# A decoder layer on one core: another form of its first two products, of its norms' sums and of its last norm's order

## The chip, the cores and the metric

The kernel runs on one core of a Trainium2 chip. The metric is the device time of one execution in microseconds (us). The engines are PE (TensorE: PE are its matmuls, PEld its weight loads), DVE (VectorE), ACT (ScalarE), POOL (GpSimd) and SP (SyncE, which here only issues DMAs). An engine takes its instructions in order and waits on semaphores for the others.

## What is computed

One layer of a decoder, for 256 prompt tokens and 8 x 4 sample tokens that share the weights (288 tokens in all, D = 2048):

```python
z = x @ w_in                       # h, gate_b, gate_c, q, k, v, g_a, g_b in one product
ya = gate_b * conv3(gate_c * h)
yb = dilated sliding-window attention(q, k, v), 3 groups of 4 heads
mixed = sigmoid(g_a) * (ya @ w_branch_a) + sigmoid(g_b) * (yb @ w_branch_b)
x1 = layernorm(ALPHA * x + mixed @ w_out, ln1_g, ln1_b)
a, b = split(x1 @ w_up)            # D_FF = 5632
y = layernorm(ALPHA * x1 + (silu(conv3(a)) * b) @ w_down, ln2_g, ln2_b)
```

`layernorm` takes mean and variance over the 2048 features of a token. Besides y the kernel returns the new caches and convolution states. All is f32.

## The kernel before, in words

Features lie on the 128 partitions, tokens in the columns: a [2048, 288] array is 16 tiles ("k") of [128, 288]. A weight block is a [2048, 128] piece of a weight matrix (1 MB), in SBUF [128, 16, 128]. A product of a block with the activations is 48 matmuls of 288 columns: both operands are split into a high part (rounded to the type F32R) and the rest, and for each k the three matmuls high x high, high x low and low x high are summed in PSUM (`mms`, L188 to L197). So a block has to be split before it is used: ACT copies it to `whi` (L137), DVE subtracts (`wlo`, L138), each in two halves of 8 tiles (`half_block`). `whi` and `wlo` have 4 half buffers each, the raw block `wst` 3 buffers.

`product` (L174) takes the split block at the head of a list, loads and splits the next one (`prepare`, L161), and returns the PSUM tile ("acc", 5 buffers). The layer is a long row of such products: 12 for q, 24 for k and v, 48 for the convolution branch, then gates, branches, w_out (16), and the FFN in three parts of 16, 16 and 12 tiles (up: two products a tile; down: 16 products a part). Attention and the work on the sample caches are put between them. The code is written in program order; a tile framework works out the semaphores, and a scheduler that simulates the times decides the order of each engine's instructions.

The start (L209 to L239): 20 matmuls of a zero tile (`N_WARM`, L212). x is loaded by ACT's queue in four pieces (`FIRST` = tiles 0-1, 2-7, 8-11, 12-15), the first two weight blocks of w_in by SP's queue, per piece first block 0, then block 1. Each piece is split as it comes (L234, L235 for weights, L200, L201 for x: `split`). The two products on them are ordinary calls of `product`. There are 8 semaphores for DMAs from these queues in turn, so the ninth DMA is issued when the first has landed. The constants `cst`, `m_dist` and the parameters `prm` are loaded in the loop over q at j == 0 (L436 to L438), that is behind the second and third block. `m_dist` lies in the array "yal".

The norms (class `Norm`, L542 to L631). dd holds the 16 tiles that are to be normalised. For tile 0, `first` gets c, the mean of tile 0's features per token, from a matmul with the constant `ones_p` (1/128; L552, an f32 matmul) and subtracts it; c is taken off all other tiles too, which keeps the sums small. `add(i)` squares a tile on ACT (L560) and adds it and its square into s1 and s2 on POOL (L564, L565). For the last tile, four f32 matmuls with `ones_d` (1/2048) sum s1, s2 and the last tile and its square over the partitions (L572, L573). At tile 14 a dummy Ln loads ACT's table ahead (L568).

`finish` (first norm, L578) computes mean, v = variance + EPS and r = exp(-0.5 ln v), with one Newton step, in SBUF tiles `lw`; the normalisation is folded into the FFN's first part (`normed`, L654), whose products read the activations unnormalised and run on while the statistics are made. `finish_out` (last norm, L593) ends the kernel: DVE and POOL share the 16 tiles, subtract the mean (`MEAN_DVE`, `MEAN_POOL`), multiply by r (`OUT_DVE`, `OUT_POOL`, L604), then ACT (L630), or DVE for the tiles in `OUT_LAST` (L628), applies g and b, and SP stores the tiles in six DMAs (`OUT_ORDER`, L631).

Of the kernel before, what the change touches and what calls it, by code (L numbers as in the profile page):

```python
# [11 lines left out]
F32R = mybir.dt.float32r  # L12
AF = mybir.ActivationFunctionType
ALU = mybir.AluOpType
# [3 lines left out]
P = 128  # L18
D = 2048
KD = D // P  # L20
# [3 lines left out]
T = SEQ + NS  # L24


H = T // 2
# [4 lines left out]
HK = KD // 2  # L32
# [18 lines left out]
C_M0 = C_TM + NT  # L51
# [11 lines left out]
N_CT = 18  # L63
N_REST = 48

FIRST = ((0, 2), (2, 6), (8, 4), (12, 4))

N_WARM = 20


N_STEP = N_CT + 2
N_STEP_BLOCKS = 2 * NG * NH + 5 * KD - 3

MEAN_DVE = ((0, 3), (3, 3), (6, 3))
MEAN_POOL = ((9, 1), (10, 2), (12, 2), (14, 2))
OUT_DVE = ((0, 1), (1, 3), (4, 3), (7, 4))
OUT_POOL = ((11, 1), (12, 2), (14, 2))
OUT_ORDER = ((0, 1), (1, 3), (4, 3), (7, 4), (11, 3), (14, 2))
OUT_LAST = (9, 10, 11, 12, 13)


@with_exitstack
def layer_kernel(ctx: ExitStack, tc: tile.TileContext, ins, outs):
# [14 lines left out]
    def sb(pl, shape, tag, dt=F32, bufs=None):  # L98
        return pl.tile(shape, dt, tag=tag, name=nm(tag), bufs=bufs)

    def acc(half=H):
        return sb(ps, [P, half, 2], "acc")

    def h2(ap):
        return ap.rearrange("p (h a) -> p h a", h=2)

    def h3(ap):
        return ap.rearrange("p k (h a) -> p k h a", h=2)

    def att(cols=512):  # L110
        return sb(ps, [P, cols], "att", bufs=2)

    def f32(ap):
        return ap.bitcast(F32)
# [9 lines left out]
    def behind(i, after):  # L124

        tc.add_manual_dep(i.ins, after.ins.name, no_sync, reason="pace")
# [47 lines left out]
    def product(x):  # L174

        w = w_ready.pop(0)
        if not w_ready:
            prepare()
        if steps_on[0]:
            spent[0] += N_STEP  # L180
            while spent[0] >= N_STEP_BLOCKS:
                spent[0] -= N_STEP_BLOCKS
                next(steps, None)
        o = acc(x[0].shape[-1])
        mms(o, w, x)
        return o.rearrange("p a h -> p h a")
# [12 lines left out]
    def split(hi, lo, src):  # L199
        act.copy(hi, src)  # L200
        dve.tensor_tensor(lo, src, f32(hi), ALU.subtract)  # L201

    ones_d = sb(big, [P, P], "ones_d")
    ones_p = sb(big, [P, P], "ones_p")
    pool.memset(ones_d, 1.0 / D)
    pool.memset(ones_p, 1.0 / P)


    zero = sb(wk, [P, T], "cy", F32R, bufs=2)  # L209
# [7 lines left out]
    xl = sb(big, [P, KD, 2, HX], "xl", F32R)  # L217
    x_in = ins["x"].rearrange("p (k t) -> p k t", t=T)
    xs = sb(big, [P, KD, T], "yah")
    for k0, n in FIRST:  # L220
        act.dma_start(xs[:, k0 : k0 + n, :], x_in[:, k0 : k0 + n, :])
    w_ready = []
    stage = []
    for b in range(2):
        stage.append((sb(wp, [P, KD, P], "wst"), ins["w_in"][b].rearrange("p (k c) -> p k c", c=P)))
        halves = [[sb(wp, [P, HK, P], n, F32R, bufs=4) for n in ("whi", "wlo")] + [HK] for _ in range(2)]
        w_ready.append(halves)
    for k0, n in FIRST:
        k = slice(k0, k0 + n)
        h = slice(k0 % HK, k0 % HK + n)  # L230
        for b, (st, src) in enumerate(stage):
            sp.dma_start(st[:, k, :], src[:, k, :])
            hi, lo, _ = w_ready[b][k0 // HK]
            act.copy(hi[:, h, :], st[:, k, :])  # L234
            dve.tensor_tensor(lo[:, h, :], st[:, k, :], f32(hi[:, h, :]), ALU.subtract)  # L235
            if b == 0:
                split(xh[:, k, :, :H], xl[:, k, :, :H], h3(xs[:, k]))
    x = (xh[:, :, :, :H], xl[:, :, :, :H])
    x_gb = (xh[:, :, :, :HG], xl[:, :, :, :HG])  # L239

    cst = sb(big, [P, C_M0], "cst")

# [187 lines left out]


    kv = sb(big, [P, 2, 2, NG, T], "dd")
    for j in range(NH):
        for g in range(NG):
            act.copy(h2(q_all[:, j, g]), product(x))
            if j == 0 and g > 0:  # L436
                for dst, src in ((cst, ins["cst"][:, :C_M0]), (m_dist, ins["cst"][:, C_M0:])) if g == 1 else ((prm, ins["prm"]),):
                    behind(sp.dma_start(dst, src), w_load[0])  # L438
        pool.tensor_copy(q_s[:, :, j, :], q_all[:, j, :, SEQ:])
    steps_on[0] = True  # L440
    for j in range(NH):
# [100 lines left out]
    class Norm:  # L542


        def __init__(self, g, b):
            self.g, self.b = g, b
            self.s1, self.s2, self.c = (lw[:, k] for k in range(3))

        def first(self):

            p = att(T)
            pe.matmul(p, ones_p, dd[:, 0], start=True, stop=True)  # L552
            act.copy(self.c, p)
            dve.tensor_tensor(dd[:, 0], dd[:, 0], self.c, ALU.subtract)

        def add(self, i):
            d = dd[:, i]
            last = i == KD - 1
            q = self.s2 if i == 0 else sb(wk, [P, T], "cy", bufs=2)
            act.activation(q, d, AF.Square)  # L560
            if i == 0:
                pool.tensor_copy(self.s1, d)
            elif not last:
                pool.tensor_tensor(self.s1, self.s1, d, ALU.add)  # L564
                pool.tensor_tensor(self.s2, self.s2, q, ALU.add)  # L565
            if i == KD - 2:

                act.activation(lw[:, 3, 0:1], q[:, 0:1], AF.Ln)  # L568
            if last:
                self.p1, self.p2 = att(T), att(T)  # L570
                for p, s, e in ((self.p1, self.s1, d), (self.p2, self.s2, q)):
                    pe.matmul(p, ones_d, s, start=True, stop=False)  # L572
                    pe.matmul(p, ones_d, e, start=False, stop=True)  # L573

        def at(self, c, i):
            return prm[:, c + i : c + i + 1]
# [1 line left out]
        def finish(self):  # L578

            mu, v, r, t = (lw[:, k] for k in range(3, 7))  # L580
            act.copy(mu, self.p1)
            act.activation(t, self.p1, AF.Square)
            dve.scalar_tensor_tensor(v, self.p2, EPS, t, ALU.add, ALU.subtract)
            act.activation(t, v, AF.Ln)
            act.activation(r, t, AF.Exp, scale=-0.5)

            dve.tensor_tensor(t, r, r, ALU.mult)
            dve.scalar_tensor_tensor(t, t, -0.5, v, ALU.mult, ALU.mult)
            dve.scalar_tensor_tensor(r, t, 1.5, r, ALU.add, ALU.mult)
            dve.scalar_tensor_tensor(mu, mu, -1.0, r, ALU.mult, ALU.mult)  # L590
            self.r, self.nmr = r, mu

        def finish_out(self, y, out):  # L593

            mu, r_pool, t = (lw[:, k] for k in range(3, 6))
            mean, v = self.p1, self.p2
            r, dev = (sb(ps, [P, T], tag, bufs=n) for tag, n in (("acc", None), ("long", 1)))
            act.activation(t, mean, AF.Square)
            act.copy(mu, mean)
            i_v = dve.scalar_tensor_tensor(v, v, EPS, t, ALU.add, ALU.subtract)  # L600

            def by_token(eng, k0, n, w, op):
                k = slice(k0, k0 + n)
                return eng.tensor_tensor(dd[:, k], dd[:, k], w.unsqueeze(1).broadcast_to([P, n, T]), op)  # L604

            for k0, n in MEAN_POOL:
                by_token(pool, k0, n, mu, ALU.subtract)
            act.activation(t, v, AF.Ln)
            act.activation(r, t, AF.Exp, scale=-0.5)
            with tc.issue_after(i_v.ins):  # L610
                for k0, n in MEAN_DVE:
                    i_m = by_token(dve, k0, n, mean, ALU.subtract)

            act.activation(t, r, AF.Square)
            with tc.issue_after(i_m.ins):
                dve.scalar_tensor_tensor(t, t, -0.5, v, ALU.mult, ALU.mult)
                i_r = dve.scalar_tensor_tensor(dev, t, 1.5, r, ALU.add, ALU.mult)
            act.copy(r_pool, dev)
            for k0, n in OUT_POOL:
                by_token(pool, k0, n, r_pool, ALU.mult)  # L620
            with tc.issue_after(i_r.ins):
                for k0, n in OUT_DVE:
                    i_m = by_token(dve, k0, n, dev, ALU.mult)
            for k0, n in OUT_ORDER:
                for i in range(k0, k0 + n):
                    if i in OUT_LAST:
                        with tc.issue_after(i_m.ins):
                            dve.tensor_scalar(y[:, i], dd[:, i], self.at(self.g, i), self.at(self.b, i), ALU.mult, ALU.add)  # L628
                    else:
                        act.activation(y[:, i], dd[:, i], AF.Identity, bias=self.at(self.b, i), scale=self.at(self.g, i))  # L630
                sp.dma_start(out[:, k0 : k0 + n, :], y[:, k0 : k0 + n, :])  # L631


    n1 = Norm(R_LN, R_LN + KD)
    for i in range(KD):
        o = product((h3(mxh), h3(mxl)))
        xf = sb(wk, [P, T], "h", bufs=2)
# [25 lines left out]

    cf = sb(big, [P, KF, 2 + 2 * NB], "qk_s")
    f = 0
    n2 = Norm(R_LN + 2 * KD, R_LN + 3 * KD)
    for part, nf in enumerate(THIRDS):
        gh = sb(big, [P, KD, T], "yah", F32R)
        gl = sb(big, [P, KD, T], "yal", F32R)
# [229 lines left out]
```

## Time and profile before

| | |
|---|---|
| runs, us | 1770.14, 1771.77, 1772.48; median 1771.77 |
| the profiled execution, us | 1772.71 |
| its span (first to last instruction), us | 1770.9 |
| mean granted TensorE clock | 0.995 |
| moved by DMA | 436.25 MB, mean 246 GB/s |
| PE matmuls L194, L195, L196 on x, busy us | 940.1, 936.3, 937.3 (3264 each) |
| DVE L138 (low parts of blocks) | 710.5 us, 580 x 1225 ns |
| ACT L137 (high parts of blocks) | 592.3 us, 580 x 1022 ns |

The times of the views are counted from the span's start; the execution's own time is 1.8 us more than the span. A group's row gives line, engine, operation, out<-in tiles, and in brackets the idle time of the engine ahead of it with what ended it. A matmul's own duration (0.29 us) is longer than the distance between two starts (0.122 us at a granted clock of 1), since they are pipelined; the second is what counts in a row of them.

### The profile page before, as it was taken

How to read it: one execution, taken by the hardware profiler on the slowest of the kernel's cores; microseconds unless marked ns; L12 is line 12 of the kernel's file. 1: busy time of each engine (PE TensorE's matmuls, PEld its weight loads, DVE VectorE, ACT ScalarE, POOL GpSimd, SP SyncE). 2: the span in 40 equal slices, each digit the busy share in tenths (PEclk: the TensorE clock that was granted, in tenths of full speed). 3: DMA queues.
4: the chain of work that ended last, by engine and by line, in shares of the span. 5: the costliest groups of instructions: out<-in, count | busy, mean ns of one | idle time of the engine just before them, and what ended most of it. 6: DMA issues, size and time to landing. Idle time of an engine off the chain costs nothing.

```text
span 1770.9 us, 33606 instructions
## 1 busy us (share of the span) xinstructions
PE 1749.3 (99%) x14277; PEld 1717.1 (97%) x14277; DVE 1010.0 (57%) x1321; ACT 800.8 (45%) x1178; POOL 252.4 (14%) x402
## 2 busy tenths in 40 slices
PE   8999999999999999999999999999999999999996
PEld 8999899999999999999999999999999999999996
DVE  4445446555645444455688787774555554555564
ACT  5444434333434333344455655553444443345444
POOL 0000000000000000001255233320011110011174
PEclk9999999999999999999999999999999999999998
DMA  8476677788787787467766566666666666666652
GB/s 305 172 301 258 258 292 272 288 304 316 260 322 301 296 322 264 151 247 270 283 218 235 214 226 226 226 226 223 229 227 226 230 222 233 219 236 219 242 191 104
DMA packets 59430, 436.25 MB, mean 246 GB/s; under 512 B 7184, under 2 KB 7696, under 8 KB 15248
## 3 DMA queue, kind: packets, MB, share of 16 engines
q1 hardware_dynamic: 57552, 428.22, 66.1%
q10 hardware_dynamic: 1728, 5.90, 0.9%
q8 instruction: 111, 1.82, 0.4%
q14 instruction: 39, 0.32, 0.0%
HBM read 389.89 MB, written 94.53 MB: 274 GB/s over the span
## 4 chain that ended last, share of the span: by engine, by line
PE 97%; ACT 1%; DVE 1%; DMA 0%; POOL 0%; issue 0%; ACTq 0%; DVEq 0%
PE acc L194 31%; PE acc L196 31%; PE acc L195 31%; PE long L356 1%; PE long L407 1%; DMA yah<-in_x 0%; PE att L283 0%; PE att L302 0%; ACT yah L630 0%; POOL qk_s L478 0%; DVE dd L604 0%; PE att L298 0%; ACT whi L137 0%; ACT xh L200 0%; PE att L276 0%
## 5 line engine op out<-in xcount | busy, mean ns | idle before, releaser
L138 DVE TENSOR_TENSOR wlo<-wst,whi 128x1024 fp32r<-128x1024 f32 (+1 forms) x580 | 710.5, 1225 | 608.0 <-ACT whi L137 602.1
L137 ACT CAST whi<-wst 128x1024 fp32r<-128x1024 f32 (+1 forms) x580 | 592.3, 1022 | 864.3 <-PE acc L195 763.6
L194 PE MATMUL acc<-xh,whi 128*128 128x288 f32 (+1 forms) x3264 | 940.1, 288 | 2.7 <-ACT whi L234 2.7
L196 PE MATMUL acc<-xh,wlo 128*128 128x288 f32 (+1 forms) x3264 | 937.3, 287 | 0.3 <-DVE wlo L235 0.3
L195 PE MATMUL acc<-xl,whi 128*128 128x288 f32 (+1 forms) x3264 | 936.3, 287 | 0.9 <-DVE xl L201 0.9
L194 PEld LDWEIGHTS acc<-xh,whi 128*128 128x128 f32 x3264 | 618.1, 189 | 14.0 <-issue 3.8
L196 PEld LDWEIGHTS acc<-xh,wlo 128*128 128x128 f32 x3264 | 618.1, 189 | 1.7 <-issue 0.8
L195 PEld LDWEIGHTS acc<-xl,whi 128*128 128x128 f32 x3264 | 618.3, 189 | 1.5 <-DVE xl L201 1.1
L194 PE MATMUL acc<-yah,whi 128*128 128x288 f32 x1216 | 348.2, 287 | 0.3 <-ACT yah L200 0.3
L196 PE MATMUL acc<-yah,wlo 128*128 128x288 f32 x1216 | 347.8, 286 | 0.0
L195 PE MATMUL acc<-yal,whi 128*128 128x288 f32 x1216 | 347.6, 286 | 0.0
L194 PEld LDWEIGHTS acc<-yah,whi 128*128 128x128 f32 x1216 | 229.7, 189 | 3.2 <-ACT h L519 2.5
L195 PEld LDWEIGHTS acc<-yal,whi 128*128 128x128 f32 x1216 | 229.8, 189 | 0.1
L196 PEld LDWEIGHTS acc<-yah,wlo 128*128 128x128 f32 x1216 | 229.8, 189 | 0.1
L478 POOL COPY qk_s<-u 128x2 f32<-128x2 f32 x44 | 41.7, 947 | 573.7 <-ACT u L680 441.5
L464 DVE SCALAR_TENSOR_TENSOR cy<-u,prm,cy 128x304 f32<-128x304 f32 x120 | 71.2, 594 | 3.3 <-ACT cy L462 0.6
L534 POOL TENSOR_TENSOR ya<-ya,dd 128x288 f32<-128x288 f32 x16 | 13.6, 849 | 306.0 <-DVE ya L533 306.0
L489 DVE TENSOR_TENSOR ya<-cy,acc 128x144 f32<-128x144 f32 x132 | 25.7, 249 | 33.0 <-PE acc L196 33.0
L478 POOL COPY cm<-u 128x2 f32<-128x2 f32 x16 | 3.0, 185 | 257.2 <-DVE u L505 257.2
L200 ACT CAST yah<-ya 128x288 fp32r<-128x288 f32 x76 | 32.7, 431 | 15.1 <-POOL ya L534 8.4
L201 DVE TENSOR_TENSOR yal<-ya,yah 128x288 fp32r<-128x288 f32 x76 | 34.9, 460 | 1.1 <-ACT yah L200 1.1
L462 ACT ACTIVATE cy<-u,prm 128x304 f32<-128x304 f32 x60 | 32.9, 549 | 3.1
(158 smaller groups left out, 791.8 us busy)
## 6 DMA issues: line engine op xcount, KB each, us to landing
wst<-in_w_in SPq DMA_DIRECT2D x114, 1024.0 KB, 6.1
wst<-in_w_up SPq DMA_DIRECT2D x88, 1024.0 KB, 4.8
wst<-in_w_down SPq DMA_DIRECT2D x32, 1024.0 KB, 4.9
cache<-in_ck SPq DMA_DIRECT2D x18, 1024.0 KB, 6.4
out_o_ck<-cache SPq DMA_DIRECT2D x18, 1024.0 KB, 9.2
cache<-in_cv SPq DMA_DIRECT2D x18, 1024.0 KB, 6.3
out_o_cv<-cache SPq DMA_DIRECT2D x18, 1024.0 KB, 9.9
wst<-in_w_a SPq DMA_DIRECT2D x16, 1024.0 KB, 4.9
```

The costliest lines, as they stand in the source:

```text
L137: act.copy(hi[:, :n, :], st[:, k0 : k0 + n, :])
L138: dve.tensor_tensor(lo[:, :n, :], st[:, k0 : k0 + n, :], f32(hi[:, :n, :]), ALU.subtract)
L194: pe.matmul(out, hi[:, c, :], xh_k, start=k == 0, stop=False)
L195: pe.matmul(out, hi[:, c, :], xl_k, start=False, stop=False)
L196: pe.matmul(out, lo[:, c, :], xh_k, start=False, stop=k == nk - 1)
L200: act.copy(hi, src)
L201: dve.tensor_tensor(lo, src, f32(hi), ALU.subtract)
L356: pe.matmul(p[j * NS : (j + 1) * NS], qm[:, j, b, :], c[:, o + j * cols : o + (j + 1) * cols], start=b == 0, stop=b == NB - 1,)
L462: act.activation(y, u[:, :YW], AF.Copy, scale=prm[:, w0 : w0 + 1])
L464: dve.scalar_tensor_tensor(y, u[:, i : i + YW], prm[:, w0 + i : w0 + i + 1], y, ALU.mult, ALU.add)
L478: pool.tensor_copy(dst[:, 0:2], u[:, SEQ : SEQ + 2])
L489: dve.tensor_tensor(a, b, c, ALU.mult)
```

## The change

At the start, x and the weights come in six pieces (2, 2, 2, 2, 4, 4 tiles). A weight piece holds the tiles of both blocks in one DMA, into arrays of their own ("dd", "yal" and the two "cache" buffers, which are used for other things later); x's last two pieces go over SP's queue. `first_two` replaces the two products: for each piece, all high x high, then high x low, then low x high, alternately for both blocks, with PE's order fixed by dependencies without semaphores. Block 2 is prepared at its beginning. There are 18 warm-up matmuls. The loads of constants move to j == 1.

In the norms, `ones_p` and `ones_d` get the type F32R. `first` takes the rounded tile 0 (a copy by ACT) for c: one matmul in the products' form. In the first norm (`tail` False) POOL adds the last tile and its square too; the sums s1 and s2 are then split in high and low, and four F32R matmuls follow. The last norm's sums stay as they were. r comes from one function, Abs_reciprocal_sqrt, instead of Ln and Exp, also in the dummy. `finish_out` alternates mean and r on DVE by groups of tiles, with r's Newton step behind the first mean operation; POOL has the mean of tiles 8 to 15 and r of 12 to 15; DVE applies g and b for tiles 8 to 11.

```diff
...
 N_CT = 18
 N_REST = 48
-FIRST = ((0, 2), (2, 6), (8, 4), (12, 4))
-N_WARM = 20
+FIRST = ((0, 2, "act"), (2, 2, "act"), (4, 2, "act"), (6, 2, "act"), (8, 4, "sp"), (12, 4, "sp"))
+N_WARM = 18
 N_STEP = N_CT + 2
 N_STEP_BLOCKS = 2 * NG * NH + 5 * KD - 3
-MEAN_DVE = ((0, 3), (3, 3), (6, 3))
-MEAN_POOL = ((9, 1), (10, 2), (12, 2), (14, 2))
-OUT_DVE = ((0, 1), (1, 3), (4, 3), (7, 4))
-OUT_POOL = ((11, 1), (12, 2), (14, 2))
-OUT_ORDER = ((0, 1), (1, 3), (4, 3), (7, 4), (11, 3), (14, 2))
-OUT_LAST = (9, 10, 11, 12, 13)
+NORM_DVE = ("m", 0, 3), ("r", 0, 3), ("m", 3, 3), ("r", 3, 3), ("m", 6, 2), ("r", 6, 2), ("r", 8, 2), ("r", 10, 2)
+MEAN_POOL = (8, 2), (10, 2), (12, 2), (14, 2)
+OUT_POOL = (12, 2), (14, 2)
+GB_DVE = (8, 9, 10, 11)
+OUT_ORDER = (0, 3), (3, 3), (6, 2), (8, 4), (12, 2), (14, 2)
 @with_exitstack
...
         act.copy(hi, src)
         dve.tensor_tensor(lo, src, f32(hi), ALU.subtract)
-    ones_d = sb(big, [P, P], "ones_d")
-    ones_p = sb(big, [P, P], "ones_p")
-    pool.memset(ones_d, 1.0 / D)
-    pool.memset(ones_p, 1.0 / P)
+    ones_d = sb(big, [P, P], "ones_d", F32R)
+    ones_p = sb(big, [P, P], "ones_p", F32R)
+    pool.memset(f32(ones_d), 1.0 / D)
+    pool.memset(f32(ones_p), 1.0 / P)
     zero = sb(wk, [P, T], "cy", F32R, bufs=2)
...
     xl = sb(big, [P, KD, 2, HX], "xl", F32R)
     x_in = ins["x"].rearrange("p (k t) -> p k t", t=T)
     xs = sb(big, [P, KD, T], "yah")
-    for k0, n in FIRST:
-        act.dma_start(xs[:, k0 : k0 + n, :], x_in[:, k0 : k0 + n, :])
     w_ready = []
-    stage = []
-    for b in range(2):
-        stage.append((sb(wp, [P, KD, P], "wst"), ins["w_in"][b].rearrange("p (k c) -> p k c", c=P)))
-        halves = [[sb(wp, [P, HK, P], n, F32R, bufs=4) for n in ("whi", "wlo")] + [HK] for _ in range(2)]
-        w_ready.append(halves)
-    for k0, n in FIRST:
+    w_two = sb(big, [P, 2, KD, P], "dd")
+    w_two_hi = sb(big, [P, 2, KD, P], "yal", F32R)
+    w_two_lo = [sb(wk, [P, 2, HK, P], "cache", F32R, bufs=2) for _ in range(2)]
+    w_in_two = ins["w_in"][0:2].rearrange("b p (k c) -> p b k c", c=P)
+    for k0, n, queue in FIRST:
         k = slice(k0, k0 + n)
-        h = slice(k0 % HK, k0 % HK + n)
-        for b, (st, src) in enumerate(stage):
-            sp.dma_start(st[:, k, :], src[:, k, :])
-            hi, lo, _ = w_ready[b][k0 // HK]
-            act.copy(hi[:, h, :], st[:, k, :])
-            dve.tensor_tensor(lo[:, h, :], st[:, k, :], f32(hi[:, h, :]), ALU.subtract)
-            if b == 0:
-                split(xh[:, k, :, :H], xl[:, k, :, :H], h3(xs[:, k]))
+        (act if queue == "act" else sp).dma_start(xs[:, k], x_in[:, k])
+        sp.dma_start(w_two[:, :, k], w_in_two[:, :, k])
+    for k0, n, _ in FIRST:
+        k = slice(k0, k0 + n)
+        split(xh[:, k, :, :H], xl[:, k, :, :H], h3(xs[:, k]))
+        split(w_two_hi[:, :, k], w_two_lo[k0 // HK][:, :, k0 % HK : k0 % HK + n], w_two[:, :, k])
     x = (xh[:, :, :, :H], xl[:, :, :, :H])
     x_gb = (xh[:, :, :, :HG], xl[:, :, :, :HG])
+    def first_two():
+        prepare()
+        o = [acc() for _ in range(2)]
+        before = None
+        for k0, n, _ in FIRST:
+            for term in range(3):
+                for k in range(k0, k0 + n):
+                    xk = x[term == 1][:, k].rearrange("p h a -> p a h")
+                    for b in range(2):
+                        w = w_two_lo[k // HK][:, b, k % HK] if term == 2 else w_two_hi[:, b, k]
+                        i = pe.matmul(
+                            o[b], w, xk, start=k == 0 and term == 0, stop=k == KD - 1 and term == 2
+                        )
+                        if before is not None:
+                            behind(i, before)
+                        before = i
+        return [t.rearrange("p a h -> p h a") for t in o]
     cst = sb(big, [P, C_M0], "cst")
...
     kv = sb(big, [P, 2, 2, NG, T], "dd")
+    q_first = first_two()
     for j in range(NH):
         for g in range(NG):
-            act.copy(h2(q_all[:, j, g]), product(x))
-            if j == 0 and g > 0:
-                for dst, src in ((cst, ins["cst"][:, :C_M0]), (m_dist, ins["cst"][:, C_M0:])) if g == 1 else ((prm, ins["prm"]),):
-                    behind(sp.dma_start(dst, src), w_load[0])
+            act.copy(h2(q_all[:, j, g]), q_first.pop(0) if q_first else product(x))
+            if j == 1:
+                dst, src = ((cst, ins["cst"][:, :C_M0]), (m_dist, ins["cst"][:, C_M0:]), (prm, ins["prm"]))[g]
+                behind(sp.dma_start(dst, src), w_load[0])
         pool.tensor_copy(q_s[:, :, j, :], q_all[:, j, :, SEQ:])
     steps_on[0] = True
     for j in range(NH):
...
     class Norm:
-        def __init__(self, g, b):
-            self.g, self.b = g, b
+        def __init__(self, g, b, tail):
+            self.g, self.b, self.tail = g, b, tail
             self.s1, self.s2, self.c = (lw[:, k] for k in range(3))
         def first(self):
+            hi = sb(wk, [P, T], "ya", F32R, bufs=2)
+            act.copy(hi, dd[:, 0])
             p = att(T)
-            pe.matmul(p, ones_p, dd[:, 0], start=True, stop=True)
+            pe.matmul(p, ones_p, hi, start=True, stop=True)
             act.copy(self.c, p)
             dve.tensor_tensor(dd[:, 0], dd[:, 0], self.c, ALU.subtract)
...
             act.activation(q, d, AF.Square)
             if i == 0:
                 pool.tensor_copy(self.s1, d)
-            elif not last:
+            elif not last or not self.tail:
                 pool.tensor_tensor(self.s1, self.s1, d, ALU.add)
                 pool.tensor_tensor(self.s2, self.s2, q, ALU.add)
             if i == KD - 2:
-                act.activation(lw[:, 3, 0:1], q[:, 0:1], AF.Ln)
+                act.activation(lw[:, 3, 0:1], q[:, 0:1], AF.Abs_reciprocal_sqrt)
             if last:
                 self.p1, self.p2 = att(T), att(T)
-                for p, s, e in ((self.p1, self.s1, d), (self.p2, self.s2, q)):
-                    pe.matmul(p, ones_d, s, start=True, stop=False)
-                    pe.matmul(p, ones_d, e, start=False, stop=True)
+                if self.tail:
+                    for p, s, e in ((self.p1, self.s1, d), (self.p2, self.s2, q)):
+                        pe.matmul(p, f32(ones_d), s, start=True, stop=False)
+                        pe.matmul(p, f32(ones_d), e, start=False, stop=True)
+                else:
+                    w = sb(wk, [P, 4, T], "cache", F32R, bufs=2)
+                    split(w[:, 0:2], w[:, 2:4], lw[:, 0:2])
+                    for k in range(4):
+                        pe.matmul((self.p1, self.p2)[k % 2], ones_d, w[:, k], start=k < 2, stop=k >= 2)
         def at(self, c, i):
             return prm[:, c + i : c + i + 1]
...
             act.copy(mu, self.p1)
             act.activation(t, self.p1, AF.Square)
             dve.scalar_tensor_tensor(v, self.p2, EPS, t, ALU.add, ALU.subtract)
-            act.activation(t, v, AF.Ln)
-            act.activation(r, t, AF.Exp, scale=-0.5)
+            act.activation(r, v, AF.Abs_reciprocal_sqrt)
             dve.tensor_tensor(t, r, r, ALU.mult)
             dve.scalar_tensor_tensor(t, t, -0.5, v, ALU.mult, ALU.mult)
...
                 k = slice(k0, k0 + n)
                 return eng.tensor_tensor(dd[:, k], dd[:, k], w.unsqueeze(1).broadcast_to([P, n, T]), op)
+            act.activation(r, v, AF.Abs_reciprocal_sqrt)
+            act.activation(t, r, AF.Square)
             for k0, n in MEAN_POOL:
                 by_token(pool, k0, n, mu, ALU.subtract)
-            act.activation(t, v, AF.Ln)
-            act.activation(r, t, AF.Exp, scale=-0.5)
-            with tc.issue_after(i_v.ins):
-                for k0, n in MEAN_DVE:
-                    i_m = by_token(dve, k0, n, mean, ALU.subtract)
-            act.activation(t, r, AF.Square)
-            with tc.issue_after(i_m.ins):
-                dve.scalar_tensor_tensor(t, t, -0.5, v, ALU.mult, ALU.mult)
-                i_r = dve.scalar_tensor_tensor(dev, t, 1.5, r, ALU.add, ALU.mult)
-            act.copy(r_pool, dev)
+            before = i_v
+            for n_op, (what, k0, n) in enumerate(NORM_DVE):
+                with tc.issue_after(before.ins):
+                    before = by_token(dve, k0, n, *((mean, ALU.subtract) if what == "m" else (dev, ALU.mult)))
+                if n_op == 0:
+                    with tc.issue_after(before.ins):
+                        dve.scalar_tensor_tensor(t, t, -0.5, v, ALU.mult, ALU.mult)
+                        before = dve.scalar_tensor_tensor(dev, t, 1.5, r, ALU.add, ALU.mult)
+                    act.copy(r_pool, dev)
             for k0, n in OUT_POOL:
                 by_token(pool, k0, n, r_pool, ALU.mult)
-            with tc.issue_after(i_r.ins):
-                for k0, n in OUT_DVE:
-                    i_m = by_token(dve, k0, n, dev, ALU.mult)
             for k0, n in OUT_ORDER:
                 for i in range(k0, k0 + n):
-                    if i in OUT_LAST:
-                        with tc.issue_after(i_m.ins):
+                    if i in GB_DVE:
+                        with tc.issue_after(before.ins):
                             dve.tensor_scalar(y[:, i], dd[:, i], self.at(self.g, i), self.at(self.b, i), ALU.mult, ALU.add)
                     else:
                         act.activation(y[:, i], dd[:, i], AF.Identity, bias=self.at(self.b, i), scale=self.at(self.g, i))
                 sp.dma_start(out[:, k0 : k0 + n, :], y[:, k0 : k0 + n, :])
-    n1 = Norm(R_LN, R_LN + KD)
+    n1 = Norm(R_LN, R_LN + KD, False)
     for i in range(KD):
         o = product((h3(mxh), h3(mxl)))
         xf = sb(wk, [P, T], "h", bufs=2)
...
     cf = sb(big, [P, KF, 2 + 2 * NB], "qk_s")
     f = 0
-    n2 = Norm(R_LN + 2 * KD, R_LN + 3 * KD)
+    n2 = Norm(R_LN + 2 * KD, R_LN + 3 * KD, True)
     for part, nf in enumerate(THIRDS):
         gh = sb(big, [P, KD, T], "yah", F32R)
         gl = sb(big, [P, KD, T], "yal", F32R)
```

## The prediction, made before the changed kernel ran

> **What bounds the kernel now.** First the page's busy rows, then who waited for whom on PE, then the stretches of the start, then the timelines of the three places that the change touches.
>
> ```profile
> PE 1749.3 (99%) x14277; PEld 1717.1 (97%) x14277; DVE 1010.0 (57%) x1321; ACT 800.8 (45%) x1178; POOL 252.4 (14%) x402
> ...
> PEclk9999999999999999999999999999999999999998
> ```
>
> PE is busy in 99% of the span: what shortens PE's stream, or lets it begin or end earlier, counts in full; what only unloads another engine does not. The page's 40 slices hide the start: one slice is 44 us. The waits of PE:
>
> ```profile
> PE acc L194 <- ACT whi L234: 2.7, 2, 1.7
> PE acc L213 <- DVE cy L210: 1.2, 1, 1.2
> PE acc L195 <- DVE xl L201: 0.9, 1, 0.9
> ```
>
> All are at the start (L234, L210, L201 run only there). So I cut the first 25 us into stretches; the columns are time, PE, PEld, DVE, ACT, POOL busy (count), granted clock, DMA share, GB/s.
>
> ```profile
> 0.00:4.40 4.40, 3.18 (x13) 3.18 (x14) 0.30 (x1) 1.42 (x2) 0.62 (x8) 1.00 0.56 141
> 4.40:7.80 3.40, 2.38 (x18) 2.17 (x17) 1.61 (x3) 1.49 (x4) 0.00 (x0) 1.00 0.99 405
> 7.80:11.20 3.40, 0.92 (x6) 0.50 (x4) 1.97 (x2) 3.28 (x3) 0.00 (x0) 1.00 1.03 411
> 11.30:14.60 3.30, 3.04 (x11) 2.72 (x12) 3.30 (x4) 2.99 (x4) 0.00 (x0) 0.50 1.06 390
> 14.70:18.00 3.30, 3.30 (x15) 3.30 (x15) 3.17 (x5) 1.24 (x2) 0.00 (x0) 0.50 1.00 409
> 18.10:25.30 7.20, 7.20 (x61) 7.20 (x61) 2.45 (x2) 2.45 (x3) 0.00 (x0) 1.00 1.00 375
> ```
>
> PE starves until 11.2 us, then the granted clock is 0.50 for 6.8 us (15 matmuls in 3.3 us, where a full clock gives 27 at 0.122 us each), and only then runs freely. The DMA is full (about 400 GB/s) throughout: the start is bounded by data, and on top of that by the halved clock. ACT's (Scalar's) timeline gives the marks; in brackets stands its idle time and what ended it:
>
> ```profile
> 14.79 1.31 ACT L234 CAST whi<-wst 128x512 fp32r<-128x512 f32 x2 [0.29 <-DMA wst<-in_w_in]
> 18.06 1.05 ACT L137 CAST whi<-wst 128x1024 fp32r<-128x1024 f32 x1 [1.96 <-DMA wst<-in_w_in]
> ...
> 25.37 0.40 ACT L435 COPY yah<-acc 128x288 f32<-128x288 f32 x1 [2.30 <-PE acc L196]
> ```
>
> The last piece of x and blocks 0 and 1 is there at about 14.75 us, block 2 at 18.0, but the second product ends only at 25.3. After that PE shows no wait to the end.
>
> **The start.** The 4.46 MB of x and two blocks stay the same, so the last piece lands at about 14.75 again. What changes is that a piece now holds tiles for both products and that PE's order follows the pieces: 2 tiles are 12 matmuls. The order of the built program puts Scalar's casts as x0, w0, w1, x1, w2, x2, w3, x3, x4, w4, x5, w5, the subtractions alike. Cumulating the GB/s column, 0.85 MB (x0, w0, x1) is there at 5.0 us and 1.70 MB (w1 to x3) at 7.1; with the half microsecond that the casts of before stood behind the bytes, w0's cast begins at 5.65 and w1's at 7.6. From there Scalar is the chain: 3 pairs of 0.62 (512 columns) and 0.67 (576) end at 11.5, then 1.15 + 1.05 + 1.15 + 1.05 (x4, w4, x5, w5) end at 15.9, just behind the data. Vector: from 8.2, 3 x (0.62 + 0.76) + 2 x (1.35 + 1.23) = 9.3, ends 17.5. PE takes group 0 at 6.3 to 7.75, group 1 at 8.9 to 10.6, group 2 to 12.1, group 3 to 13.6, group 4 (24 matmuls, 2.9 us) 13.7 to 16.6, group 5 to 19.5. Block 2 has the same bytes ahead of it: cast at 18.06, 1.05, then Vector's 1.23 gives its low half at 20.4, and the product's third matmul waits for it, so the third product counts as begun at 20.1 (if block 2 comes a microsecond sooner, 19.5). Before: 25.3. **Minus 5.3** (5.2 to 5.8), if the clock stays up.
>
> Will it? Before, the clock fell after a 3.4 us stretch in which PE was 27% busy by its rows (0.92 of 3.40), and stayed up after one of 70% (2.38). By my times the new stretch 7.8 to 11.2 is busy about 60%, the next one over 95%. I take it that 60% is enough; nothing in the trace between 27% and 70% shows it. The Trainium skill ("TensorE: Matmul & The Clock Gate", Part 1, What's actually happening) has the clock halved after an idle window of about 3.4 us and restored after one busy window, the windows running free of the kernel's start. By that rule no gap here (1.2 us at most) would halve it, and the sum stays; the trace is harsher, since before's longest gap is 1.9 us and the halving lasted 6.8 us, two such windows.
>
> The constants cst, m_dist and prm are loaded some products later. In Scalar's order prm's first use stands behind the copy of product 4 (about 37 us), its load behind block 6's at about 22 us; loads of before took 8 to 9 us to land. m_dist's tile now holds the two blocks' high halves, so its load waits on SP's queue until the second product ends (20 us), with block 6 and prm behind it; block 6 is used from about 43 us. Nothing else waits. The two warm-up matmuls left out lie in PE's idle time; cost nothing.
>
> **The norms.** The chain of waits shows what PE spends in the sums:
>
> ```profile
> 886.53 0.48 PE att L552 x2
> 972.28 0.97 PE att L572 x4
> 975.34 0.48 PE att L573 x2
> 976.69 0.48 PE att L573 x2
> ```
>
> One f32 matmul is two records, 0.48 us; one in the products' form is 0.12. *first()*, twice: 2 x (0.48 - 0.12) = **minus 0.7**. The added copy by Scalar reads dd 0, ready at 884.1 and 1687.2, and stands in Scalar's order right behind a cast ending 884.6 and 1686.7; PE reaches the matmul at 887 and 1689.7, so it does not wait. First norm's sums: 1.93 us become 4 x 0.12: **minus 1.45**. They are moved 41 matmuls (5 us) later in PE's order; the two last GpSimd additions (0.8 each), the split (0.66 + 0.76) end at about 976.3, PE comes by at 977.7, no wait. The statistics are then ready at about 982.9 instead of 981.95 (one table load of 1.28 and one pass of 0.44 less, but begun 2 us later), while PE is 1.45 ahead. Behind these steps queue Scalar's casts and Vector's low halves for the FFN's second and third pairs; they were ready 2.9 to 3.6 us before PE used them, so 0.5 to 1.2 us is left: no stall, up to 1 us if I am wrong.
>
> **The end.** The last norm's matmuls stay as they are. After them:
>
> ```profile
> 1758.08 0.45 DVE L616 SCALAR_TENSOR_TENSOR cache<-cache,att 128x288 f32<-128x288 f32 x1
> ...
> 1759.48 3.65 DVE L604 TENSOR_TENSOR dd<-dd,long 128x288 f32<-128x288 f32 x4 [0.46 <-ACT cache L618]
> 1759.97 0.63 ACT L630 ACTIVATE yah<-dd,prm 128x288 f32<-128x288 f32 x1 [0.52 <-DVE dd L604]
> 1760.63 6.10 SPq L631 DMA_DIRECT2D out_o_y<-yah x6
> ```
>
> Now, from Vector's v at 1755.3: reciprocal root 1755.7, its square 1756.2, first mean operation (3 tiles, 0.97) 1756.2, two small ones to 1757.1, Scalar's copy (which Vector waited for before, and by its semaphore does again) 1757.6, r for tiles 0 to 2 at 1758.6. Scalar begins its g and b at 1758.65 instead of 1759.97, has 12 tiles of 0.52 instead of 11, and waits for Vector at tile 3 (1760.6): it ends at 1765.4 instead of 1766.2. GpSimd has 12 tiles as before, Vector ends at 1764.6. The last DMA is 288 KB as before. **Minus 0.85**; bounds 0 (one more wait of Scalar) and 1.6 (Scalar never waits).
>
> **Sum:** -5.3 - 0.7 - 1.45 - 0.85 = -8.3, from the profiled execution's 1772.71 us: 1764.4. That execution lies 0.94 above the median of before's runs (1771.77); from the median it is **1763.5**.
>
> **Rivals.**
> *Half the start's gain (chance 0.24).* The clock is halved at 11.25 once more for 6.8 us. About 30 of 96 matmuls are done by then, 28 more at 0.24 by 18.1, 38 at 0.122 end at 22.7: minus 2.6 instead of 5.3, 1766.2. A weight piece in 1 KB packets that lands 2.5 us later gives the same. For it: 60% is between the known points. Against: no gap as long as before's.
> *The start gains nothing (0.09).* PE must now follow a fixed order and could stand behind each piece; the second product still ends near 25. Then only the norms and the end count: -3.0, 1768.8. Against: both orders wait for the same last piece at 14.75, and half of the 10.5 us behind it is the clock.
> *Slower (0.05).* PE takes the pieces in trickles and the clock stays at half far beyond 18 us. Each us at half costs 0.5; if all runs at half from 6.3 on, the start loses to before's from about 27 us, and pays for the other 3.0 and 0.2% more from about 34. Halved to 38.6 it is about 5.8 over before: 1777.6. Against: back-to-back matmuls ended the halving after 6.8 us.
> *More (0.02):* block 2 earlier and the end's full 1.6: 1761.5.
>
> **Numbers.** Forecast 0.60. The range 1761.5 to 1768.0 takes in the first rival and the bounds of the end and of the FFN's possible stall; it leaves out the third case and the slower one. 0.2% (3.5 us), about what can be told from no change here, puts the border at 1768.2: faster 0.60 + 0.24 + 0.02 = 0.86, same 0.09, slower 0.05.
>
> **What would show it.** The second product's copy by Scalar near 20 us instead of 25.4; granted clock 1.00 in all stretches after 4.4 us; block 2's cast near 18 as before; the sums at 0.12 us a matmul with no PE wait around them; Scalar's last g and b about 0.8 us nearer to PE's last matmul. Wrong would be: a 0.50 clock row, a wait of PE for Scalar or Vector after 25 us, or a last weight piece that lands after 16 us.

## The result, and the profile after

The changed kernel takes 1765.20 us (median of 6 runs, 1765.03 to 1765.58) where the kernel before, run beside it, takes 1771.58 (6 runs, 1770.14 to 1772.48): a ratio of 0.9965, interval 0.9954 to 0.9977, 6.4 us. The forecast was 1763.5, its range 1761.5 to 1768.0. The profiled execution took 1765.03 us (span 1763.2, mean granted clock 0.997) against 1772.71 (1770.9, 0.995).

First the start. Three of the stretches of the changed kernel, with the columns of the prediction's table (time, PE, PEld, DVE, ACT, POOL busy, granted clock, DMA share, GB/s):

```profile
7.80:11.20 3.40, 2.79 (x17) 2.15 (x17) 2.30 (x5) 2.12 (x5) 0.00 (x0) 1.00 1.04 385
11.30:14.60 3.30, 3.30 (x28) 3.30 (x29) 3.21 (x4) 2.88 (x4) 0.00 (x0) 1.00 1.08 416
14.70:18.00 3.30, 3.30 (x29) 3.30 (x28) 2.77 (x3) 1.68 (x3) 0.00 (x0) 1.00 1.00 415
```

The stretch that had 6 matmuls has 17, the two that ran at 0.50 run at 1.00, with 28 and 29 matmuls instead of 11 and 15; the DMA was as full before. ACT's timeline gives the marks:

```profile
15.17 1.05 ACT L201 CAST yal<-dd 128x1024 fp32r<-128x1024 f32 x1 [0.19 <-DMA dd<-in_w_in]
17.64 1.99 ACT L138 CAST whi<-wst 128x1024 fp32r<-128x1024 f32 x2 [1.43 <-DMA wst<-in_w_in]
19.68 0.70 ACT L452 COPY yah<-acc 128x288 f32<-128x288 f32 x2
```

The last weight piece is cast at 15.17 and waited only 0.19 us for its data, block 2 is cast at 17.64, and both products are copied at 19.68 (before: 25.37). Events that are the same in both programs lie 5.30 us apart from here to the attention (140.26 and 134.96, 276.33 and 271.02).

Now the waits of PE over the whole span; the columns are the wait's total, how many, and the longest:

```profile
PE acc L214 <- DVE cy L211: 1.2, 1, 1.2
PE acc L197 <- DVE wlo L139: 0.6, 1, 0.6
PE acc L249 <- ACT xh L201: 0.6, 2, 0.4
PE acc L195 <- ACT yah L201: 0.3, 1, 0.3
```

L214 and L249 are the start, and the last row, between 1000 and 1300 us, is one that the kernel before has too (0.3 us as well). The second row is new, and it is not at the start: it lies at 1706, in the last part of the FFN, and the prediction has no such wait. Three engines show how it comes about, POOL, ACT and DVE in turn:

```profile
1683.73 15.97 POOL L730 TENSOR_TENSOR dd<-dd,cache 128x288 f32<-128x288 f32 x14 [13.54 <-ACT cache L573]
...
1700.79 0.79 POOL L585 TENSOR_TENSOR cache<-cache,cy 128x288 f32<-128x288 f32 x1
```

```profile
1701.61 0.44 ACT L580 ACTIVATE cy<-dd 128x288 f32<-128x288 f32 x1 [4.26 <-POOL cache L585]
...
1703.47 1.55 ACT L138 CAST whi<-wst 128x1024 fp32r<-128x1024 f32 x2
```

```profile
1704.53 1.91 DVE L139 TENSOR_TENSOR wlo<-wst,whi 128x1024 fp32r<-128x1024 f32 x1 [5.48 <-ACT whi L138]
```

As soon as the last norm's c exists, POOL subtracts it from 14 tiles in one go (16 us), from the 15th after tile 0's copy, and only then adds the first square. ACT's next square needs one of the two "cy" buffers, so it waits 4.26 us for that addition, and a second square behind it again; the cast of the next weight block stands behind both in ACT's order, DVE's low half behind the cast, PE behind the low half:

```profile
1706.50 0.39 PE L197 MATMUL acc<-yah,wlo 128*128 128x288 f32 x1 [0.61 <-DVE wlo L139]
1706.72 0.29 PE L195 MATMUL acc<-yah,whi 128*128 128x288 f32 x1
```

The matmul ahead of these began at 1705.60. From there to 1706.72 PE takes 1.12 us for two distances of 0.122, so against a full row it loses 0.88 us here. Most of this comes with the low half itself, which took 1.91 us instead of the usual 1.23 while POOL worked through its additions beside it: at 1.23 it would have been there 0.7 us earlier, and by this estimate PE would have lost about 0.2. The kernel before has the same 14 subtractions (15.67 us from 1690.67) and the same wait of ACT, but there the order is the other way round:

```profile
1702.73 1.05 ACT L137 CAST whi<-wst 128x1024 fp32r<-128x1024 f32 x1 [2.31 <-PE acc L195]
1707.50 0.44 ACT L560 ACTIVATE cy<-dd 128x288 f32<-128x288 f32 x1 [3.72 <-POOL cache L565]
```

The cast came first, and the wait cost nothing. Nothing in the diff touches these lines; the scheduler, with other times, sorted them otherwise.

At the end, ACT's timeline of the changed kernel:

```profile
1752.14 1.67 ACT L653 ACTIVATE yah<-dd,prm 128x288 f32<-128x288 f32 x3 [1.12 <-DVE dd L629]
1754.19 4.77 ACT L653 ACTIVATE yah<-dd,prm 128x288 f32<-128x288 f32 x9 [0.39 <-DVE dd L629]
```

It applies g and b to 12 tiles, waits once at tile 3 and ends 10.70 us behind Vector's v (1748.26), where it ended 11.42 us behind it before. From v to the end of the span it is 14.94 us instead of 16.09.

The account between the two profiled executions: start -5.30, first norm with its first() -1.77 (the difference grows from 5.30 to 7.08 by the FFN), second first() -0.36, the new wait +0.88, the end -1.15: together -7.7; measured -7.7.

### The profile page after: what moved, and what is told of

It is laid out like the page before. It is cut to its first block, busy times and chain, and to the rows that moved or that the text cites. A ratio compares the mean times of both kernels' runs of the same rounds, so it can differ in the third digit from the quotient of the medians.

```text
span 1763.2 us, 33588 instructions
## 1 busy us (share of the span) xinstructions
PE 1745.2 (99%) x14269; PEld 1712.9 (97%) x14269; DVE 1010.2 (57%) x1322; ACT 798.9 (45%) x1178; POOL 254.0 (14%) x403
## 4 chain that ended last, share of the span: by engine, by line
PE 96%; POOL 1%; ACT 1%; DVE 1%; DMA 0%; issue 0%; SPq 0%; ACTq 0%; DVEq 0%
PE acc L195 31%; PE acc L197 31%; PE acc L196 31%; PE long L372 1%; PE long L423 1%; POOL dd L730 1%; PE acc L249 0%; PE att L299 0%; PE att L318 0%; DMA dd<-in_w_in 0%; ACT whi L138 0%; POOL qk_s L495 0%; ACT yah L653 0%; DVE dd L629 0%; PE att L314 0%
## 5 line engine op out<-in xcount | busy, mean ns | idle before, releaser
L195 PE MATMUL acc<-xh,whi 128*128 128x288 f32 (+1 forms) x3232 | 929.1, 287 | 0.0
L197 PE MATMUL acc<-xh,wlo 128*128 128x288 f32 (+1 forms) x3232 | 926.8, 287 | 0.0
L196 PE MATMUL acc<-xl,whi 128*128 128x288 f32 (+1 forms) x3232 | 925.7, 286 | 0.0
L195 PEld LDWEIGHTS acc<-xh,whi 128*128 128x128 f32 x3232 | 610.9, 189 | 10.7 <-issue 3.8
L197 PEld LDWEIGHTS acc<-xh,wlo 128*128 128x128 f32 x3232 | 610.9, 189 | 1.2 <-issue 0.8
L196 PEld LDWEIGHTS acc<-xl,whi 128*128 128x128 f32 x3232 | 610.9, 189 | 0.3 <-issue 0.2
L584 POOL TENSOR_TENSOR cache<-cache,dd 128x288 f32<-128x288 f32 x29 | 27.9, 964 | 49.1 <-DVE dd L669 33.6
```

The source lines that it names most:

```text
L195: pe.matmul(out, hi[:, c, :], xh_k, start=k == 0, stop=False)
L196: pe.matmul(out, hi[:, c, :], xl_k, start=False, stop=False)
L197: pe.matmul(out, lo[:, c, :], xh_k, start=False, stop=k == nk - 1)
```

## The experiments

Ratios are to the kernel before, run beside them. The theory: start, norms and end add up, the clock at the start is kept by the small pieces, and the new wait comes from ACT's order. The rivals were that warm-up matmuls keep the clock, that the piece sizes matter only through the clock, and that GpSimd is simply too slow for its additions.

**The start alone.** The kernel before with the new FIRST and N_WARM, first_two and the loads at j == 1, and its old norms.

> Before with the change's start alone (pieces for both blocks, fixed PE order, 18 warm-up matmuls, constants at j == 1); the norms as before. The profile after shows fixed points of PE's stream 5.3 us earlier right behind the start (140.26 against 134.96), so the theory that the start is worth 5.3 us against an execution with the clock halved for 6.8 us expects a span of 1765.6, granted clock 1.00 in all stretches after 6 us, and a median 4 to 5.3 us under before's (before's profiled execution was 1.1 us above its median). Rival: the start's gain needs the norms' changes (shared buffers, other order by the scheduler): less than 3 us.

1767.59 us (1767.42 to 1767.83, 11 runs), ratio 0.9978 (0.9969 to 0.9987): -3.9 by medians. The clock is full from 4.14 us on, and the wait at 1706 is absent.

**The norms and the end alone.** The changed kernel with the old start.

> After with the start of before: the norms' changes alone. Expected from the two traces: first() -0.36, first norm's sums and first() -1.8, the end -1.15 (from the last norm's v to the span's end 16.09 against 14.94), together -3.3 us; if the wait of PE near tile 4 of the last norm (0.8 us, after only) comes from the norms' changes, it is here too and leaves -2.5. Rival: that wait belongs to the start's shift in time and is absent: -3.3.

1768.82 us (1767.26 to 1770.40, 11 runs), ratio 0.9983 (0.9974 to 0.9992): -2.7 by medians. With the start alone that is -6.6, against -6.4 measured: the parts add up. The wait at 1706 is there, 0.6 us, so it comes with the norms' part and not with the start. The clock in this profile was a surprise:

```profile
11.30:14.60 3.30, 3.01 (x11) 2.69 (x12) 3.30 (x4) 3.00 (x4) 0.00 (x0) 0.51 1.06 375
14.70:18.00 3.30, 3.30 (x29) 3.30 (x28) 3.24 (x5) 1.24 (x2) 0.00 (x0) 0.99 1.00 412
```

The program of the start is that of before, whose second row had 15 matmuls at 0.50; here the halving lasted 3.41 us instead of 6.83. Its runs stand in groups (1767.3 to 1767.6, 1768.8 to 1769.2, 1770.4), as do the 27 runs of the kernel before beside it (about 1769.9, 1771.5 and 1772.6; 4, 17 and 6). Each run's mean granted clock goes with its group: 0.997 in the four fastest runs here, 0.996 in the middle ones, 0.995 in the slowest. One window of 3.41 us at half takes 0.001 off that mean. The length of the halved stretch is not a property of the code alone.

**Coarse pieces.** The changed kernel, with x and weights in the pieces of before; all of x is back on ACT's queue with it, which no run tests by itself:

```diff
-FIRST = ((0, 2, "act"), (2, 2, "act"), (4, 2, "act"), (6, 2, "act"), (8, 4, "sp"), (12, 4, "sp"))
+FIRST = ((0, 2, "act"), (2, 6, "act"), (8, 4, "act"), (12, 4, "act"))
```

> After with the pieces of before's sizes (tiles 0-1, 2-7, 8-11, 12-15, all of x on ACT's queue), still both blocks in one DMA and PE's fixed order. If small pieces are what keeps the clock up: PE stands from about 7 us until the 6-tile piece is split (9.5 to 10.5), the clock is 0.50 for 6.8 us as in before, the second product ends at 22 to 23 instead of 19.6 and the time is 2.5 to 3.4 us over after. Rival: the fixed order over both blocks is what counts, PE catches up behind the last piece: at most 1 us over after.

1771.35 us (1770.10 to 1772.02, 11 runs), ratio 0.9999 (0.9990 to 1.0007): 6.2 over the changed kernel, about twice what was expected and more than the whole start had gained. PE's wait for the piece of six tiles, and two stretches:

```profile
PE acc L249 <- ACT xh L201: 4.9, 1, 4.9
```

```profile
7.80:11.20 3.40, 0.20 (x2) 0.00 (x0) 0.00 (x0) 1.40 (x2) 0.00 (x0) 1.00 1.02 413
...
14.70:18.00 3.30, 3.30 (x15) 3.30 (x15) 3.30 (x4) 2.91 (x4) 0.00 (x0) 0.50 1.02 421
```

PE stands idle for almost a whole stretch, and the clock is at 0.50 for 6.83 us from 11.88. The fixed order with these pieces gains nothing; with the small pieces it does. How much of it is the clock and how much the data, the next two split.

**Coarse pieces with PE kept busy.** The kernel above with 36 matmuls of the zero tile between its first and second group; they add nothing to the results.

```diff
+            if k0 == 0:
+                fill = att(T)
+                for _ in range(N_FILL):
+                    i = pe.matmul(fill, zero[:, :P], zero, start=True, stop=True)
+                    behind(i, before)
+                    before = i
```

> The coarse-pieces kernel (1771.35 us; PE stood 4.9 us for the 6-tile piece, clock 0.50 for 6.8 us) with 36 matmuls of the zero tile put into PE's order in that pause; they add nothing to the outputs. If the halved clock is a cost of its own, the clock stays at 1.00 and the kernel gets faster by about 3 us through more work: 1768.3. Rival: the pause and the late data are the whole cost: 1771.4 or more.

1769.45 us (1769.24 to 1771.36, 11 runs), ratio 0.9991 (0.9982 to 1.0000): 1.9 less than without them, by more work on PE. The clock stays up where it was 0.50:

```profile
7.80:11.20 3.40, 3.40 (x28) 3.40 (x27) 0.00 (x0) 1.07 (x1) 0.00 (x0) 1.00 1.00 402
...
14.70:18.00 3.30, 2.91 (x24) 2.69 (x23) 3.30 (x4) 3.30 (x5) 0.00 (x0) 1.00 1.00 417
```

The second product still ends at 24.25, not at 19.6: ACT and DVE get their big pieces later, and PE waits for them. It begins its second group at 13.19 with 84 of 96 matmuls to go. So of the 6.2 us the halved clock is about 1.9 at most runs, and the size of the pieces at a full clock the other 4.3.

**The same with 16 matmuls**, to leave a stretch partly busy.

> The coarse-pieces kernel with 16 instead of 36 zero matmuls in the pause of PE (2.0 us of about 5). The clock's stretches of 3.4 us run free of the kernel's start, so the one that holds the rest of the pause is busy for something like a third to two thirds. If that share is enough, the clock stays at 1.00 and the time is that of 36 matmuls (1769.45); if not, it is halved and the time is that of none (1771.35). A mixture over the executions would show that the phase decides.

1770.94 us (1769.06 to 1772.36, 11 runs), ratio 0.9998 (0.9989 to 1.0006): inconclusive as a time, a mixture. Its profile is not:

```profile
7.80:11.20 3.40, 1.95 (x15) 1.72 (x14) 0.00 (x0) 0.20 (x1) 0.00 (x0) 1.00 1.01 396
11.30:14.60 3.30, 0.54 (x3) 0.54 (x4) 2.10 (x2) 3.30 (x3) 0.00 (x0) 0.97 1.07 411
14.70:18.00 3.30, 3.30 (x16) 3.30 (x16) 3.30 (x3) 3.30 (x5) 0.00 (x0) 0.53 0.99 410
```

A stretch of 57% (1.95 of 3.40) was followed by one of 16% (0.54 of 3.30), and then the clock was halved for 3.41 us, from 14.39 to 17.81. So the limit below which it falls isn't pinned down: 57% alone did not bring it down at once. (The halving from 14.39 to 17.81 gives the borders of the clock's own windows; cut there, the shares are 64% and 10%.)

**No warm-up.** The changed kernel with N_WARM = 1.

> After with 1 warm-up matmul instead of 18. Theory: the clock starts halved and comes up only when a stretch of about 3.4 us was busy; the first groups (5.9 to about 12 us) run at 0.24 us a matmul, PE falls 2 to 3.5 us behind the data and the whole run is that much longer than after, 1767.2 to 1768.7. Rival: PE waits for data there anyway and catches up by the last piece: within 0.5 us of after.

1765.32 us (1764.98 to 1765.81, 6 runs), ratio 0.9967 (0.9955 to 0.9979): 0.1 over the changed kernel. The theory of 1767.2 or more falls. PE's timeline:

```profile
5.88 1.32 PE L249 MATMUL acc<-xh,yal 128*128 128x288 f32 x4 [4.05 <-ACT yal L201]
...
18.80 1.14 PE L249 MATMUL acc<-xh,cache 128*128 128x288 f32 x8
```

The clock is halved until 10.08, as the theory had it, but the first groups then merely fill the time in which PE would have waited for the next piece. From 5.88 PE runs without a gap and ends the second product at 19.8, 0.2 later.

**POOL's order.** In the changed kernel the subtraction of c from tile i is queued on POOL behind the additions of tile i - 2 (pool_last holds each add's last instruction):

```diff
-                    pool.tensor_tensor(dd[:, i], dd[:, i], n2.c, ALU.subtract)
+                    with tc.issue_after(pool_last[max(i - 2, 0)].ins) if i > 1 else ExitStack():
+                        pool.tensor_tensor(dd[:, i], dd[:, i], n2.c, ALU.subtract)
...
-                n2.add(i)
+                pool_last.append(n2.add(i))
```

> After with GpSimd's subtraction of c from tile i (last norm) queued behind the additions of tile i - 2, so that 14 subtractions no longer stand ahead of the first addition. Theory: ACT's square for tile 3 waited 4.26 us for GpSimd's addition, ACT's cast of a block stood behind it, DVE's low half behind that, PE waited 0.8 us; all gone: 0.6 to 0.8 us under after, no wait of PE for DVE's wlo after 25 us. Rival: the wait only moves to the next place where ACT waits for GpSimd (tiles 1 to 3): within 0.2 us of after.

1764.28 us (1764.20 to 1764.32, 5 runs), ratio 0.9959 (0.9947 to 0.9972): 0.92 under the changed kernel. POOL's timeline:

```profile
1688.44 1.78 POOL L734 TENSOR_TENSOR dd<-dd,cache 128x288 f32<-128x288 f32 x1
1690.18 1.25 POOL L585 TENSOR_TENSOR cache<-cache,dd 128x288 f32<-128x288 f32 x1
```

Subtraction and addition alternate, ACT's squares wait only for DVE there (0.5 to 1.3 us), and PE's wait at 1706 is gone. The low half that was late comes in time, and in 1.23 us:

```profile
1700.90 1.23 DVE L139 TENSOR_TENSOR wlo<-wst,whi 128x1024 fp32r<-128x1024 f32 x1 [2.18 <-ACT whi L138]
```

POOL has the same work, so its amount of work was not the cause; its order was. The order acts in two ways that this run undoes together, by what waits on ACT and by what POOL does beside Vector's low half; how much each is worth was not tested apart.

**Sums in f32.** The changed kernel with first() on the f32 tile and the first norm's sums as in the last.

> After with the means c and the first norm's sums as f32 matmuls, as before. PE's records: 2 x (0.48 - 0.12) + (1.93 - 0.49) = 2.2 us more in a stream without waits: 1767.4. The wait of PE near tile 4 of the last norm may stay or go with the scheduler's order, 0.8 us: 1766.6 if it goes. Rival: the matmuls of another form are hidden: within 0.3 us of after.

1766.36 us (1766.24 to 1766.82, 8 runs), ratio 0.9972 (0.9962 to 0.9982): 1.2 over the changed kernel. The wait at 1706 is absent here; with the 0.9 us that it costs, the f32 matmuls cost 2.0 to 2.1, against the 2.15 that the prediction gave them. That the wait is absent shows again that it hangs on the scheduler's order.

**Ln and Exp for r.** The changed kernel with the old pair in both norms and Ln in the dummy:

```diff
-            act.activation(r, v, AF.Abs_reciprocal_sqrt)
+            act.activation(t, v, AF.Ln)
+            act.activation(r, t, AF.Exp, scale=-0.5)
```

> After with exp(-0.5 ln v) by Ln and Exp in both norms, as before, in after's order. In the end's chain from v to the Newton step stand then one more pass (0.41 us) and one more table load (1.28 us) ahead of Vector's second small operation, and Vector's order is fixed behind it: the theory expects 1.2 to 1.7 us over after, all of it behind PE's last matmul. Rival: Scalar's g and b pass or GpSimd bound the end, the load is hidden: under 0.3 us.

1766.89 us (1766.68 to 1767.19, 10 runs), ratio 0.9976 (0.9967 to 0.9985): 1.7 over the changed kernel. ACT's and DVE's timelines:

```profile
1749.60 1.28 ACT L633 ACT_TABLE_LOAD   x1
```

```profile
1751.78 0.46 DVE L644 SCALAR_TENSOR_TENSOR cache<-cache,att 128x288 f32<-128x288 f32 x1 [1.69 <-ACT cache L634]
```

Exp needs another table than Ln, loaded on the path: 1.28 and one more pass of 0.41 are the 1.69 for which Vector waits. The Trainium skill ("ScalarE: Activation LUTs", Table sets: the hidden batching unit) has Ln and then Exp in one set, with one load; in this trace each has its own.

**POOL's order, and the copy of r later.** As above, with ACT's copy of r for POOL written behind Vector's first multiplication by r:

```diff
+                if n_op == 1:
+                    act.copy(r_pool, dev)
```

> The GpSimd-order kernel (1764.28 us) with Scalar's copy of r for GpSimd written behind Vector's first multiplication by r. In after that multiplication stood 0.47 us behind the copy, though it needs nothing from it; both read the same PSUM tile. Theory: the framework orders the two readers of the tile as written; with the order turned round Vector's chain at the end is 0.47 us shorter, and Scalar's g and b with it: 1763.8 to 1763.9. Rival: Scalar is held by its own row of 12 tiles or by GpSimd: 1764.3.

1763.90 us (1763.74 to 1763.97, 5 runs), ratio 0.9959 (0.9945 to 0.9973): 0.38 under the same kernel without the move, and the fastest of all, 1.3 under the changed kernel. DVE's first multiplication at 1749.86 follows its Newton step (1749.37, 0.46 us) without a wait; in the changed kernel it waits 0.47 us for the copy, though both only read.

## Why the prediction was right, and where it was wrong

- *The start, -5.3: right to the digit against the profiled execution* (-5.30). The last casts (15.9 forecast, 15.17 + 1.05 = 16.2), the second product's end (19.5; 19.6) and the third's start (20.1; 19.6, or 19.9 with its two short gaps counted) came as worked out. What came otherwise: the stretch 7.8 to 11.2 was busy for 82% (2.79 of 3.40), not 60%, since PE's first groups came earlier (w0's cast at 5.27, not 5.65; w1's at 6.64, not 7.6). The point in doubt, whether 60% is enough, was therefore never put to the test by the change. That half of the 10.5 us behind the last piece was the clock, as the second rival was answered, is too much: 6.83 us at half a clock lose 3.4 us at most.
- *The clock.* The Trainium skill ("TensorE: Matmul & The Clock Gate", Part 1, What's actually happening) has windows of about 3.4 us that run free of the kernel's start. The trace agrees: halved stretches of 3.41 and 6.83 us, one or two windows, for one and the same start. That section speaks of an idle window and does not say how idle; here the halving followed stretches in which PE was busy for 27% (before) and 34% (1.15 of 3.40, norms alone). Cut at the windows' own borders, as the beginnings and ends of the halvings give them (11.25 and 18.08 in before), the last window ahead of a halving was busy for 26% in before, 31% in the norms alone, 10% with 16 zero matmuls and not at all with coarse pieces, and a window of 64% left the clock up. If the last window decides, the limit lies between 31% and 64%, and the prediction's 60% lay within that gap, settled by no run. What makes one window of it or two stays open: the first halved window was busy for 92% both in before, where a second followed, and in the norms alone, where none did.
- *The warm-up, 18 for 20, at nothing: right.* Even 17 fewer cost 0.1.
- *first() and the first norm's sums, -0.7 and -1.45: right.* -0.36 twice, and -1.77 - (-0.36) = -1.41. PE waited nowhere at the sums, though the statistics came later than worked out (978.65, which is 984.3 when the 5.66 us are added by which PE was ahead; forecast 982.9). The f32 experiment gives them 2.0 to 2.1 together.
- *The FFN: no stall, 0.5 to 1.2 us left: right for the first norm's FFN;* behind 25 us PE waits only for the 0.3 us that the kernel before has too, and at 1706.
- *The step that failed: for the last norm's first(), "PE reaches the matmul at 887 and 1689.7, so it does not wait".* A wait of PE for Scalar or Vector after 25 us was among the prediction's own signs of being wrong, and it came. That step looked at the one matmul and its copy. It didn't look at what the same c sets off next on POOL, the 14 subtractions, nor at what is queued on ACT behind the square that waits for them. It costs 0.88; undoing only POOL's order gives 0.92 back. The rows were all there in before, ACT's wait of 3.72 us included; only its order against one cast was luck.
- *The end, -0.85: right mechanism, mis-sized.* -1.15: ACT's part is -0.72, close to what was worked out; the last DMA's issue came 0.36 us behind ACT's end instead of 0.50, and the stretch from it to the end of the span fell from 4.17 to 3.88 us, which no step had. Why these are shorter isn't settled; one profile of each cannot tell it from chance.
- *From the profile to the median, -0.94: failed.* The sum against the profiled execution (1764.4) missed the profiled execution (1765.03) by 0.6. The prediction then carried before's offset over, as if it belonged to every kernel. But before's executions spread over 2.3 us and more, the changed kernel's over 0.55. The profiles show from where such a spread can come: the halved stretch lasts two windows (before, coarse pieces), one (norms alone, 16 zero matmuls) or none (36 zero matmuls). The mean clock of each execution bears it out as far as three digits go: of the 27 runs of before, the 4 of the fastest group have 0.996 and the 6 of the slowest 0.995. That each of before's longer executions is one with two windows is argued from this, not shown, since only profiled executions show when the clock was halved. A kernel whose start never halves has no such spread, and nothing to subtract. Most of the miss is here: 0.94 of 1.7, then 0.6 from the two steps above, and 0.17 by which the changed kernel's profile lies under its median.

## What to carry to other kernels

Where a start is bound by data, cut the first pieces to what the engine that uses them can do while the next piece comes, and have each piece carry everything that a group of matmuls needs: that was worth 6 us here, two thirds of it without the clock. When a change makes a value ready earlier or later, follow everything that waits for it on every engine, and whose queue that stands in: an engine that is busy for 14% of the time stopped PE through two others. Before an offset between a profile and a median is carried over, ask whether the change removes its cause.

## What the runs showed of the hardware that was not expected

- One and the same start had its clock halved for 3.41 us in one kernel's execution and 6.83 us in another's, and the times of unchanged kernels fall into groups some 1 to 1.6 us apart.
- 17 fewer warm-up matmuls cost 0.1 us where the data come slower than PE at half its clock uses them, and 36 useless matmuls in a pause gained 1.9 us where a pause was followed by a full row of work.
- Vector's pass over [128, 1024] took 1.91 us beside a row of additions on GpSimd, and 1.23 us for the same block where GpSimd was idle; by the estimate above, most of PE's loss at 1706 comes with it.
- ACT's pass with Abs_reciprocal_sqrt shared its table with the squares and copies around it: 5 table loads in the whole kernel with it, 7 with Ln and Exp.
